# Four plain block products at the entry of a ConvFFN, a swapped transpose, and a norm and its squares in another place

## The chip, the cores and the metric

The kernel runs on one core of one Trainium2 chip. The metric is device time in microseconds (us), lower is better. An execution's own time holds its profiled span and about 2 us around it. The engines: PE (TensorE, matmuls), DVE (VectorE), ACT (ScalarE), POOL (GpSimd) and SP (SyncE, which issues the DMAs). PSUM is the memory that matmuls write.

## The reference

A two-layer streaming encoder step on 1056 tokens (1024 of a prompt, 32 of a sample), width 1024. Layer 0 mixes with an HGRN2 gated recurrence of 8 heads, layer 1 with differential attention. What matters here is what stands around the mixer `m` in each layer:

```
x = x + rmsnorm(m, g_norms[i, 1])
h = rmsnorm(x, g_norms[i, 2])
g, u = split(h @ w_ffn_in[i])              # 1024 -> 2 * 2816
c = conv_b + conv_w[0]*g[t-2] + conv_w[1]*g[t-1] + conv_w[2]*g[t]
f = (silu(c) * u) @ w_ffn_out[i]           # 2816 -> 1024
x = x + rmsnorm(f, g_norms[i, 3])
x = x + sigmoid(x @ w_ple_gate[i]) * (ple[i] @ w_ple[i])
```

`rmsnorm` divides by the root of a mean of squares over the 1024 features of a token. After layer 0, x is normed again and projected to the keys and values that layer 1 reads.

## The kernel before, in words

**Products.** Activations stand feature-major: eight tiles of 128 features by tokens. Every float32 factor is split in a rounded high part (ACT casts, L169) and the rest (DVE subtracts, L170; L110 and L111 for weight pieces of 1024 columns), and a product is three matmuls: high by high, low by high, high by low (L120 to L122). Weights come by DMA into a `raw` tile and are split into `ws` slabs. Tokens go in groups of 384, 384 and 288 (t = 0, 1, 2), in the FFN in two halves of 528, each in two pieces of 264.

**The mixer's output** (`mixer_out`, both layers). A unit (t, j) is the product for one feature tile j of token group t; its PSUM is added to a partial sum by DVE (L304), or for t = 2 copied by ACT (L302). ACT then squares it and POOL adds the square into `acc` (L195 to L203). `norm_m(t)` turns the sum into a factor with a matmul by ones (L190) and two ACT operations, multiplies the eight tiles (L318), adds the residual (L319) and squares again into `xacc`; `norm_x(t)` multiplies by that second factor (L331) and writes the `y` tiles, the FFN's input. PE's order here is written out by hand: the units, with the norms' ones-matmuls between them, and behind them `ple`, the product of the per-layer embedding, which needs none of the norms. The order on the other engines comes from a scheduler, which sets an instruction as early as its inputs are there, by priority.

**The FFN's entry** (`operands`, `weights7`, `ffn_in`). Input and weights are cut into two by two blocks, and each of the 22 blocks of 128 FFN rows (ft) takes seven products in the manner of Strassen and Winograd instead of eight. The input's seven operands are four blocks or sums of them (b1, b2, b3 and b6, b7, b5, b4), made once per layer by DVE (L432, L433, L434, L439) and split by ACT and DVE; the seven weight operands are made for each ft. A product is 24 matmuls of 264 columns. Results leave PSUM by ACT copies (L513, L528) and DVE adds (L505). `raw` has two buffers for these weights, there are ten slabs, and PSUM pools of 3 (`psd`), 4 (`psm`) and 1 (`psr`).

**The FFN's end** (`ffn_out`). `post` norms f, `gate` multiplies the embedding by a sigmoid and adds (L629 to L636), and `store(t)` splits the new x for the next layer and squares it into `xacc`, whose ones-matmul (L181) gives the factor of the next norm.

**The HGRN heads** (`gla`, layer 0). Each head ends its score stage with the 32 tokens of the sample: a 32x32 matmul into PSUM tile `ps` (L987), a masked copy of it by DVE (L988), a transpose of the keys by PE into another part of the same tile (L989), and an ACT copy of that (L991).

Of the kernel before, what the change touches and what calls it, by code (L numbers as in the profile page):

```python
# [18 lines left out]
P = 128  # L19
# [27 lines left out]
class Trunk:  # L47
# [228 lines left out]
    def mixer_out(self, l, wsrc, gpost, resid, yp):  # L276

        nc, tc, io = self.nc, self.tc, self.io
        with tc.tile_pool(name=self.nm("mo"), bufs=1, reuse_waits="tile") as mp:
# [6 lines left out]
            for ks in ((4, 5, 6, 7), (0, 1, 2, 3)):  # L286
                for i in (1, 2):
                    for k in ks:
                        y[k][i] = yp.tile([P, YT[i][1]], F32, tag=f"y{k}{i}", name=self.nm("y"))
            for k in range(KD):  # L290
                y[k][0] = yp.tile([P, YT[0][1]], F32, tag=f"y{k}0", name=self.nm("y"))
            g_in = self.G(4 * l + 2)

            def unit(t, j):
# [39 lines left out]
            with tc.manual_schedule(engines={mybir.EngineType.PE}):  # L334
                for t, j in [(t, j) for t in range(3) for j in range(KD)]:
# [50 lines left out]
    def layer_end(self, l, wsrc, gpost, resid, last):  # L386

        tc = self.tc
        with self.phase("ff", 1, 2, m=4, r=1) as fp:
            with tc.tile_pool(name=self.nm("yp"), bufs=1, reuse_waits="tile") as yp:  # L390
# [4 lines left out]
                w = self.weights7(l, 0)  # L395
                b = next(b)
            with tc.tile_pool(name=self.nm("rp"), bufs=1, reuse_waits="tile") as rp:
                ready = self.ffn_in(l, w, b, fp, rp)
# [6 lines left out]
    def operands(self, y):  # L405
# [5 lines left out]
        def alloc(op, ps):  # L411
            for p in ps:
                out[p] = [[op.tile([P, HT], F32R, tag=f"b{p}{k}{i}", name=self.nm(f"b{p}")) for i in range(2)]
                          for k in range(4)]
# [5 lines left out]
        def b(kh, hf, k, i):  # L420
            return y[4 * kh + k][1 + i] if hf else y[4 * kh + k][0][:, parts[i]]

        def put(p, kh, hf, i=None):
            for k in range(4):
                c = slice(0, HT) if i is None else parts[i]
                self.split(y[4 * kh + k][0] if i is None else b(kh, hf, k, i), *[o[:, c] for o in out[p][k]])

        def sums(i):
            put(3, 1, 1, i)
            for k in range(4):  # L430
                b11, b12, b22 = b(0, 0, k, i), b(0, 1, k, i), b(1, 1, k, i)
                nc.vector.tensor_tensor(b11, b12, b11, SUB)  # L432
                nc.vector.tensor_tensor(b12, b22, b12, SUB)  # L433
                nc.vector.tensor_tensor(b22, b22, b11, SUB)  # L434
# [954 lines left out]
```

## Time and profile before

| | |
|---|---|
| median of 3 runs | 3009.33 us (2995.96 to 3010.63) |
| the profiled execution's own time | 3011.07 us |
| its span | 3009.3 us |
| PE busy | 2906.3 us, 97% |
| DVE busy | 2001.6 us, 67% |
| ACT busy | 1299.2 us, 43% |
| POOL busy | 283.8 us, 9% |
| mean granted TensorE clock | 0.983 |

A busy PE is not PE at its full clock: the granted clock of a stretch stands beside its busy time. Where PE is idle the trace names what it waited for last. The core is one, so the span is the time but for the 2 us around it.

### The profile page before, as it was taken

What the parts mean: (1) busy time and instruction counts of PE and PEld (TensorE: products, weight loads), DVE (VectorE), ACT (ScalarE), POOL (GpSimd) and SP (SyncE); (2) the same over time, 40 slices, a digit from 0 to 9 for tenths busy, and PEclk for the clock granted to TensorE, in tenths of its full rate; (3) what the DMA queues carried; (4) which work ended last, traced back from release to release, by engine and by line L of the source; (5) the groups of instructions that cost most, each with busy time, mean ns of one, the idle gap of its engine ahead of it and who ended that gap; (6) DMA issues with size and microseconds to landing.
All of it is one profiled execution on the core that took longest, in us unless ns stands there. A gap on an engine that the chain in (4) does not pass through costs nothing.

```text
span 3009.3 us, 50595 instructions
## 1 busy us (share of the span) xinstructions
PE 2906.3 (97%) x20302; PEld 2798.5 (93%) x20302; DVE 2001.6 (67%) x3874; ACT 1299.2 (43%) x2355; POOL 283.8 (9%) x431
## 2 busy tenths in 40 slices
PE   8999999988999999999989999999889999999999
PEld 8889999978999999998988888989889999999989
DVE  7556555488777766667657575575887777767674
ACT  6445435464343333115436454565643333331151
POOL 0000000140000000003321111001400000000020
PEclk9999999999999999999999999999889999999999
DMA  3111111351222224334232232232512222242242
GB/s 133 46 39 41 53 47 60 103 172 64 85 72 79 85 79 137 124 117 148 87 107 77 84 92 81 90 105 74 184 57 79 79 79 79 83 152 86 86 148 70
DMA packets 105013, 275.34 MB, mean 91 GB/s; under 512 B 12241, under 2 KB 49225, under 8 KB 104777
## 3 DMA queue, kind: packets, MB, share of 16 engines
q1 hardware_dynamic: 102216, 263.71, 26.2%
q0 software_dynamic: 2560, 8.39, 1.4%
q8 instruction: 159, 2.61, 0.4%
q14 instruction: 78, 0.63, 0.1%
HBM read 196.53 MB, written 71.86 MB: 89 GB/s over the span
## 4 chain that ended last, share of the span: by engine, by line
PE 85%; DVE 8%; ACT 3%; issue 1%; DMA 1%; POOL 1%; SPq 0%; DVEq 0%; ACTq 0%; POOLq 0%
PE psm L122 14%; PE psm L120 14%; PE psm L121 14%; PE psd L120 11%; PE psd L121 11%; PE psd L122 11%; PE po L1233 1%; DVE b L170 1%; PE pss L1199 1%; PE psm L1225 1%; PE pss L1200 1%; DVE ws L111 1%; DVE x L170 1%; PE po L1235 1%; PE po L181 1%
## 5 line engine op out<-in xcount | busy, mean ns | idle before, releaser
L120 PE MATMUL psd<-x,ws 128*128 128x384 f32 (+1 forms) x1512 | 518.9, 343 | 17.7 <-ACT x L681 9.9
L120 PE MATMUL psm<-b,ws 128*128 128x264 f32 x1760 | 502.2, 286 | 4.4 <-ACT y L528 2.5
L122 PE MATMUL psm<-b,ws 128*128 128x264 f32 x1760 | 503.7, 287 | 2.2 <-DVE ws L170 2.2
L121 PE MATMUL psm<-b,ws 128*128 128x264 f32 x1760 | 502.7, 286 | 2.8 <-DVE b L170 2.8
L121 PE MATMUL psd<-x,ws 128*128 128x384 f32 (+1 forms) x1512 | 498.5, 330 | 0.0
L122 PE MATMUL psd<-x,ws 128*128 128x384 f32 (+1 forms) x1512 | 494.4, 327 | 1.3 <-DVE ws L111 1.3
L121 PE MATMUL psm<-y,ws 128*128 128x384 f32 (+1 forms) x1056 | 342.5, 325 | 5.6 <-DVE y L170 5.6
L120 PE MATMUL psm<-y,ws 128*128 128x384 f32 (+1 forms) x1056 | 343.7, 326 | 0.4 <-DVE f L612 0.3
L122 PE MATMUL psm<-y,ws 128*128 128x384 f32 (+1 forms) x1056 | 341.2, 324 | 0.0
L120 PEld LDWEIGHTS psm<-b,ws 128*128 128x128 f32 x1760 | 333.5, 190 | 5.8 <-ACT y L528 3.0
L121 PEld LDWEIGHTS psm<-b,ws 128*128 128x128 f32 x1760 | 333.7, 190 | 3.5 <-DVE b L170 3.5
L122 PEld LDWEIGHTS psm<-b,ws 128*128 128x128 f32 x1760 | 333.4, 190 | 2.6 <-DVE ws L170 2.6
L169 ACT CAST ws<-raw 128x512 fp32r<-128x512 f32 x308 | 191.1, 621 | 326.1 <-DVE raw L479 105.3
L612 DVE TENSOR_TENSOR f<-psm,f 128x384 f32<-128x384 f32 (+1 forms) x432 | 221.1, 522 | 153.5 <-PE psm L122 152.4
L120 PEld LDWEIGHTS psd<-x,ws 128*128 128x128 f32 x1512 | 288.8, 191 | 30.4 <-ACT x L681 10.1
L121 PEld LDWEIGHTS psd<-x,ws 128*128 128x128 f32 x1512 | 288.9, 191 | 6.8
L122 PEld LDWEIGHTS psd<-x,ws 128*128 128x128 f32 x1512 | 288.3, 191 | 6.7 <-issue 3.2
L170 DVE TENSOR_TENSOR ws<-raw,ws 128x512 fp32r<-128x512 f32 x308 | 211.2, 697 | 114.6 <-ACT ws L169 114.6
L111 DVE TENSOR_TENSOR ws<-raw,ws 128x1024 fp32r<-128x1024 f32 (+1 forms) x138 | 166.6, 1208 | 93.3 <-ACT ws L110 93.0
L120 PE MATMUL psd<-b,ws 128*128 128x264 f32 x704 | 200.1, 285 | 17.0 <-ACT b L169 17.0
L121 PEld LDWEIGHTS psm<-y,ws 128*128 128x128 f32 x1056 | 199.6, 189 | 7.8 <-DVE y L170 7.0
L120 PEld LDWEIGHTS psm<-y,ws 128*128 128x128 f32 x1056 | 199.4, 189 | 2.5 <-DVE f L612 1.0
(303 smaller groups left out, 6093.4 us busy)
## 6 DMA issues: line engine op xcount, KB each, us to landing
raw<-wfi SPq DMA_DIRECT2D x88, 512.0 KB, 3.3
hd<-y SPq DMA_DIRECT2D x44, 528.0 KB, 2.7
raw<-wfo SPq DMA_DIRECT2D x44, 512.0 KB, 4.4
rh<-hd SPq DMA_DIRECT2D x40, 528.0 KB, 3.7
raw<-wia SPq DMA_DIRECT2D x30, 512.0 KB, 3.4
ped<-pe SPq DMA_DIRECT2D x16, 528.0 KB, 2.8
y<-ped SPq DMA_DIRECT2D x16, 528.0 KB, 4.8
raw<-wpg SPq DMA_DIRECT2D x16, 512.0 KB, 4.3
```

Of the source, the lines that this page charges most:

```text
L111: nc.vector.tensor_tensor(wl[:, w], raw[:, w], wh[:, w].bitcast(F32), SUB)
L120: mm(ps, wh, xh, start=start and i == 0, stop=False, skip_group_check=more)
L121: mm(ps, wh, xl, start=False, stop=False, skip_group_check=more)
L122: mm(ps, wl, xh, start=False, stop=stop and i == n - 1, skip_group_check=more)
L169: self.nc.scalar.copy(hi, src)
L170: self.nc.vector.tensor_tensor(lo, src, hi.bitcast(F32), SUB)
L181: nc.tensor.matmul(ps, self.ones, acc, start=True, stop=True)
L612: nc.vector.tensor_tensor(f[j][t], ps, f[j][t], ADD)
L1199: mm(ps[:, :pad], qs[c][:, P * i:P * i + P], kh[c][:, k0:k0 + pad], start=True, stop=False)
L1200: mm(ps[:, :pad], qs[c][:, P * i:P * i + P], kl[c][:, k0:k0 + pad], start=False, stop=True)
L1225: nc.tensor.transpose(ps[:, i * P:i * P + P], ws[a][:, kt * P:kt * P + P], self.ident)
L1233: mm(po, v[:, 2 * b, :], wts[b][:, 0:256], start=b == 0, stop=False)
```

## The change

- **Entry.** Block ft = 0 is computed as eight plain block products (four blocks for the gate, four for the up rows), on operands b1, b2, b3 and b5 alone; gate and up rows have PSUM tiles and copies of their own. Its weights are two plain pieces in four slabs, and the seven operands of ft = 1 are loaded before it. The other 21 blocks keep the seven products.
- **Operands.** The four feature tiles of a block lie in one tile, so a split or a subtraction is one instruction over 2112, 960 or 1152 elements. The splits of b1 and b2 have high priority, and the sums come in another order: b5 first, then b6, b7, b4.
- **Mixer's output.** The evacuations of `unit` have high priority; `norm_x(0)` stands behind unit (2, 3) instead of (1, 7).
- **Rows.** The FFN's rows are eight named tiles, taken in turn, instead of a pool of eight.
- **FFN's end.** The squares for the next norm are made in `gate`, not in `store`; for the last two feature tiles of t = 2 DVE adds them instead of POOL; `store(2)` has high priority.
- **Short chunk.** The transpose is issued ahead of the masked copy.

```diff
--- mixer_out
                 if t == 2:
                     nc.tensor.matmul(ps, self.ident, m, start=False, stop=True)
                     m = y[j][2]
-                    nc.scalar.copy(m, ps)
-                else:
-                    nc.vector.tensor_tensor(m, ps, m, ADD)
                 with tc.high_priority():
+                    if t == 2:
+                        nc.scalar.copy(m, ps)
+                    if t < 2:
+                        nc.vector.tensor_tensor(m, ps, m, ADD)
                     self.sumsq(acc[t], m, j == 0, mp)
...
-                    if (t, j) == (1, 7):
-                        norm_x(0)
                     if (t, j) == (2, 1):
                         norm_m(1)
+                    if (t, j) == (2, 3):
+                        norm_x(0)
--- layer_end
-                w = self.weights7(l, 0)
+                w = [self.piece(self.io["wfi"][l, i]) for i in (0, NFF)]
+                w1 = self.weights7(l, 1)
--- operands
-        put(1, 0, 0)
-        put(2, 1, 0)
-        sums(0)
-        sum4(0)
-        yield
-        sums(1)
+        with self.tc.high_priority():
+            put(1, 0, 0)
+            put(2, 1, 0)
+        put(3, 1, 1, 0)
+        yield
         self.opb = self.right("opb", 1)
         alloc(self.opb, (7, 5, 4))
+        put(3, 1, 1, 1)
+        sub((0, 0), (0, 1), (0, 0))
+        put(5, 0, 0)
+        sub((0, 1), (1, 1), (0, 1))
+        sub((1, 1), (1, 1), (0, 0))
+        for i in range(2):
+            put(6, 1, 1, i)
+        sub((1, 0), (1, 0), (1, 1))
         for i in range(2):
             put(7, 0, 1, i)
-        put(5, 0, 0)
-        sum4(1)
         put(4, 1, 0)
--- ffn_in, block ft = 0
+                gp, u = row(), row()
+                halo(gp, cv)
+                X, Y = ([self.psm()[:, 0:HT // 2] for _ in range(2)] for _ in range(2))
+                Z, W = ([(self.psd() if m == "d" else self.psm(m))[:, 0:HT // 2] for m in mk] for mk in ("dd", "dr"))
...
+                block(0, 0, 1, X)
+                copies([(p1[:, n], X[s]) for s, n in enumerate(pieces)])
+                block(1, 0, 1, Y)
+                copies([(q1[s], Y[s]) for s in range(2)])
+                block(0, 1, 2, X, more=True)
+                block(1, 1, 2, Y, more=True)
+                block(0, 1, 3, Z)
+                block(1, 1, 3, W)
+                block(0, 0, 5, Z, more=True)
+                block(1, 0, 5, W, more=True)
+                copies([(gp[:, 2 + n.start:2 + n.stop], X[s]) for s, n in enumerate(pieces)])
+                copies([(u[:, n], Y[s]) for s, n in enumerate(pieces)])
+                u2 = p1
+                for s, n in enumerate(pieces):
+                    add(u[:, HT + n.start:HT + n.stop], W[s], q1[s])
--- ffn_out, gate and store
             nc.sync.dma_start(dst[j][:, t0:t0 + n], f[j][t])
+            if not last:
+                self.sumsq(self.acc[t], f[j][t], j == 0, f2, nc.vector if t == 2 and j >= 6 else None)
...
-                self.store_x(t, j, f[j][t], self.acc[t], f2)
+                self.store_x(t, j, f[j][t], None, f2)
--- rows of ffn_in and ffn_out
-            return rp.tile([P, T + 4], F32, tag="y", name=self.nm("y"), bufs=8)
+        self.nrow += 1
+        return pool.tile([P, T + 4], F32, tag=f"y{self.nrow % 8}", name=self.nm("y"), bufs=1)
--- gla
         mm(ps[0:32, 0:32], kd[:, SEQ:T], qd[:, SEQ:T], start=True, stop=True)
+        nc.tensor.transpose(ps[0:32, P:2 * P], kc[:, SEQ:T], self.ident)
         nc.vector.copy_predicated(A[0:32, SEQ:T], tri[0:32], ps[0:32, 0:32])
-        nc.tensor.transpose(ps[0:32, P:2 * P], kc[:, SEQ:T], self.ident)
```

Lines of the changed kernel are shifted (L304 is L306, L318 and L319 are L319 and L320, L331 is L332, L989 is L1025, and both copies of PSUM at the entry of block 0 are L501).

PE at the short chunk of a head in layer 0, before. `psm_951` is the tile that the 32x32 product and the transpose share; `psd_965` belongs to a projection of the next head.

```order
L122 MATMUL psd_897<-x_65_217,ws_712 128x384
L987 MATMUL psm_951<-qd_596,d_517 32x32
L989 MATMUL psm_951<-ident,f_483 32x128 [waits DMAHW5_49,DVE_49]
L999 MATMUL psm_957<-ident,f_483 128x128 x4
L120 MATMUL psd_965<-x_18_123,ws_711 128x288
L121 MATMUL psd_965<-x_19_124,ws_711 128x288
```

The same place after:

```order
L122 MATMUL psd_897<-x_65_217,ws_712 128x384
L1024 MATMUL psm_951<-qd_596,d_517 32x32
L1025 MATMUL psm_951<-ident,f_483 32x128 [waits DMAHW5_49]
L1036 MATMUL psm_957<-ident,f_483 128x128 x4
L120 MATMUL psd_965<-x_18_123,ws_711 128x288 [waits DVE_49]
L121 MATMUL psd_965<-x_19_124,ws_711 128x288
```

The order of PE's instructions is the same; the transpose no longer waits for DVE, and a wait for DVE (an earlier one, for the PSUM buffer of `psd_965`) stands two instructions later.

DVE in `mixer_out` of layer 0 before, from the end of `norm_m(0)` (L318, L319) over the evacuations of units of t = 1 (L304, one per `psd`) to the first multiplication of `norm_x(0)` (L331):

```order
L318 SCALAR_TENSOR_TENSOR x_663_4987<-x_663_4987,gc,psm_5674 128x384
L319 TENSOR_TENSOR x_659_4965<-x_659_4965,x_842_5708 128x384
L318 SCALAR_TENSOR_TENSOR x_715_5276<-x_715_5276,gc,psm_5674 128x384
L319 TENSOR_TENSOR x_663_4987<-x_663_4987,x_844_5716 128x384
L318 SCALAR_TENSOR_TENSOR x_717_5291<-x_717_5291,gc,psm_5674 128x384
L304 TENSOR_TENSOR x_687_5093<-psd_5757,x_687_5093 128x384
L319 TENSOR_TENSOR x_715_5276<-x_715_5276,x_846_5724 128x384
L319 TENSOR_TENSOR x_717_5291<-x_717_5291,x_848_5732 128x384
L304 TENSOR_TENSOR x_690_5118<-psd_5774,x_690_5118 128x384
L304 TENSOR_TENSOR x_692_5138<-psd_5791,x_692_5138 128x384
L304 TENSOR_TENSOR x_719_5306<-psd_5808,x_719_5306 128x384
L331 SCALAR_TENSOR_TENSOR y_5497<-x_645_4864,gc,psm_5842 128x384
```

The same place after, up to the first multiplication of `norm_m(1)` (`psm_5859`):

```order
L306 TENSOR_TENSOR x_687_5093<-psd_5739,x_687_5093 128x384
L320 TENSOR_TENSOR x_647_4886<-x_647_4886,x_818_5666 128x384
L319 SCALAR_TENSOR_TENSOR x_649_4915<-x_649_4915,gc,psm_5656 128x384
L319 SCALAR_TENSOR_TENSOR x_655_4943<-x_655_4943,gc,psm_5656 128x384
L306 TENSOR_TENSOR x_690_5118<-psd_5756,x_690_5118 128x384
L320 TENSOR_TENSOR x_649_4915<-x_649_4915,x_820_5674 128x384
...
L306 TENSOR_TENSOR x_721_5321<-psd_5807,x_721_5321 128x384
L320 TENSOR_TENSOR x_717_5291<-x_717_5291,x_830_5714 128x384
L111 TENSOR_TENSOR ws_5477<-raw_5475,ws_5476 128x1024
L319 SCALAR_TENSOR_TENSOR x_667_5011<-x_667_5011,gc,psm_5859 128x384
```

The evacuations stand between the operations of `norm_m(0)` instead of behind them, and `norm_m(1)` follows at once, with `norm_x(0)` behind it.

ACT from the end of block 0 to the start of block 1 of the FFN in layer 0, before. `b_...` are operands, `ws_...` weight slabs, `y_6607` is the gate's row of block 0, `p_1034` the copy of block 1's first product.

```order
L169 CAST b_1007_6536<-y_5503 128x528
L169 CAST b_1009_6538<-y_5504 128x528
L528 COPY y_6607<-psm_6580 128x264
L528 COPY y_6607<-psm_6581 128x264
L169 CAST ws_6793<-raw_6786 128x512
L169 CAST ws_6792<-raw_6786 128x512
L169 CAST ws_6790<-raw_6785 128x512
L169 CAST ws_6795<-raw_6785 128x512
L513 COPY p_1034_6840<-psm_6814 128x264
```

The same place after. `b_955` is b4's high part, `ws_6394` the last slab of ft = 1, `raw_6883` a weight tile of ft = 2, `y_6448` and `y_6449` the gate's and up's rows of block 0.

```order
L169 CAST b_908_6194<-y_5483 128x4x288
L169 CAST ws_6394<-raw_6384 128x512
L169 CAST b_955_6420<-y_5485 128x2112
L169 CAST ws_6887<-raw_6883 128x512
L169 CAST ws_6889<-raw_6883 128x512
L501 COPY y_6448<-psm_6452 128x264
L501 COPY y_6449<-psm_6454 128x264
L501 COPY y_6448<-psm_6453 128x264
L501 COPY y_6449<-psm_6455 128x264
L501 COPY p_974_6704<-psm_6678 128x264
```

The copies that empty block 0's first PSUM tiles stand behind b4's cast and behind two casts of weights of ft = 2; `psm_6678`, the first product of block 1, uses the PSUM buffer that `y_6448<-psm_6452` empties.

## Rows read from the trace of the kernel before

**Rows 1.** Page, busy us of each engine, share of the span, instructions

```profile
PE 2906.3 (97%) x20302; PEld 2798.5 (93%) x20302; DVE 2001.6 (67%) x3874; ACT 1299.2 (43%) x2355; POOL 283.8 (9%) x431
```

**Rows 2.** Waits of PE: line, engine and line waited for, us in total, times, longest

```profile
PE psd L120 <- ACT b L169: 17.0, 2, 8.5
PE psm L989 <- DVE A L988: 10.7, 8, 4.6
...
PE psd L120 <- DVE x L304: 7.2, 2, 3.6
PE psm L181 <- POOL xacc L203: 6.4, 1, 6.4
...
PE psd L120 <- ACT y L302: 5.1, 2, 2.6
...
PE psd L120 <- ACT pe L378: 3.7, 2, 1.9
PE psm L190 <- POOL acc L203: 3.0, 2, 1.5
```

**Rows 3.** Stretches: us, busy us (instructions) of five engines, granted clock, DMA

```profile
710.00:1110.00 400.00, 400.00 (x3280) 400.00 (x3279) 290.12 (x511) 156.27 (x255) 18.44 (x76) 1.00 0.22 78
1510.00:1515.00 5.00, 1.22 (x3) 0.94 (x4) 4.31 (x9) 3.93 (x7) 3.22 (x2) 0.50 0.39 146
155.00:160.00 5.00, 4.90 (x18) 4.80 (x19) 2.08 (x12) 3.22 (x5) 0.00 (x0) 0.50 0.00 0
160.00:165.00 5.00, 5.00 (x37) 5.00 (x36) 4.04 (x4) 3.34 (x5) 0.00 (x0) 0.89 0.00 0
90.00:95.00 5.00, 5.00 (x32) 4.98 (x31) 1.91 (x3) 4.21 (x5) 0.00 (x0) 0.72 0.00 0
635.00:640.00 5.00, 3.01 (x9) 2.38 (x10) 4.93 (x6) 2.97 (x8) 3.67 (x3) 0.55 0.32 95
680.00:690.00 10.00, 6.88 (x28) 6.26 (x29) 10.00 (x27) 5.47 (x13) 0.00 (x0) 0.50 0.11 41
```

**Rows 4.** Timeline of PE, `mixer_out` of layer 0 to block 1: start, us, [idle before]

```profile
617.53 0.81 PE L190 MATMUL psm<-acc,ones 128*128 128x384 f32 x2
...
666.03 0.28 PE L120 MATMUL psm<-b,ws 128*128 128x264 f32 x1
666.15 0.29 PE L121 MATMUL psm<-b,ws 128*128 128x264 f32 x1
...
705.01 0.29 PE L120 MATMUL psm<-b,ws 128*128 128x264 f32 x1
```

**Rows 5.** Timeline of DVE, the norms, then subtractions and splits at the entry, layer 0

```profile
615.09 3.24 DVE L331 SCALAR_TENSOR_TENSOR y<-x,gc,psm 128x384 f32<-128x384 f32 x6 [1.62 <-ACT psm L192]
618.25 1.22 DVE L111 TENSOR_TENSOR ws<-raw,ws 128x1024 fp32r<-128x1024 f32 x1
...
632.97 1.10 DVE L319 TENSOR_TENSOR x<-x,x 128x384 f32<-128x384 f32 x1 [0.94 <-DMA x<-xT]
...
644.19 0.94 DVE L318 SCALAR_TENSOR_TENSOR y<-y,gc,psm 128x288 f32<-128x288 f32 x2
...
676.46 1.35 DVE L439 TENSOR_TENSOR y<-y,y 128x240 f32<-128x240 f32 x4
...
690.94 1.56 DVE L439 TENSOR_TENSOR y<-y,y 128x288 f32<-128x288 f32 x4
692.41 2.56 DVE L170 TENSOR_TENSOR b<-y,b 128x528 fp32r<-128x528 f32 x4
694.89 0.69 DVE L170 TENSOR_TENSOR ws<-raw,ws 128x512 fp32r<-128x512 f32 x1
```

**Rows 6.** Timeline of ACT, casts of operands at the entry, layer 0

```profile
691.47 2.23 ACT L169 CAST b<-y 128x528 fp32r<-128x528 f32 x4 [5.70 <-issue]
...
705.94 0.38 ACT L513 COPY p<-psm 128x264 f32<-128x264 f32 x1 [1.25 <-PE psm L122]
```

**Rows 7.** Page, DMA issues: queue, count, KB each, median us from issue to landing

```profile
raw<-wfi SPq DMA_DIRECT2D x88, 512.0 KB, 3.3
```

More of the change, by code (lines that the diff above doesn't have):

```diff
@@ L285, in mixer_out @@
             y = [[None] * 3 for _ in range(KD)]
[L286 to L291, printed above, removed]
+            self.y3 = {}
+            for i in (1, 2, 0):
+                for kh in (1, 0):
+                    g = self.y3[kh, i] = yp.tile([P, 4, YT[i][1]], F32, tag=f"y{kh}{i}", name=self.nm("y"))
+                    for k in range(4):
+                        y[4 * kh + k][i] = g[:, k, :]
             g_in = self.G(4 * l + 2)
@@ L481, in weights7, with row, ffn_in, copies @@
         return out
-    def ffn_in(self, l, a, b, fp, rp):
+    def row(self, pool):
+        self.nrow += 1
+        return pool.tile([P, T + 4], F32, tag=f"y{self.nrow % 8}", name=self.nm("y"), bufs=1)
+    def ffn_in(self, l, w0, a, b, fp, rp):
         nc, tc = self.nc, self.tc
         pieces = [slice(0, HT // 2), slice(HT // 2, HT)]
+        n0, n1 = pieces
+        e = SEQ - HT - n1.start
         def row():
-            return rp.tile([P, T + 4], F32, tag="y", name=self.nm("y"), bufs=8)
+            return self.row(rp)
+        def copies(pairs):
+            with tc.high_priority():
+                for out, ps in pairs:
+                    nc.scalar.copy(out, ps)
+        def halo(gp, cv):
+            nc.gpsimd.memset(gp[:, 0:2], 0.0)
+            nc.gpsimd.tensor_copy(gp[:, 1026:1028], cv[:, 4:6])
         for ft in range(NFF):
-            a = self.weights7(l, ft) if ft else a
+            a = self.weights7(l, ft) if ft > 1 else a
             cv = self.ffc[:, l, ft, :]
@@ L500, in prod @@
                     self.mm3(ps[s], [(w[:, k * P:k * P + P], w[:, 512 + k * P:512 + k * P + P],
-                                      b[p][k][0][:, n], b[p][k][1][:, n]) for k in range(4)], not more, True, more)
+                                      b[p][0][:, k, n], b[p][1][:, k, n]) for k in range(4)], not more, True, more)
             def add(out, ps, other):
@@ L505, in add @@
                     nc.vector.tensor_tensor(out, ps, other, ADD)
-            X = [self.psm()[:, 0:HT // 2] for _ in range(2)]
-            prod(1, X)
-            p1 = fp.tile([P, HT], F32, tag="p1", name=self.nm("p1"))
-            gp = row()
-            with tc.high_priority():
-                for s, n in enumerate(pieces):
-                    nc.scalar.copy(p1[:, n], X[s])
-            nc.gpsimd.memset(gp[:, 0:2], 0.0)
-            nc.gpsimd.tensor_copy(gp[:, 1026:1028], cv[:, 4:6])
-            Y = [self.psm()[:, 0:HT // 2] for _ in range(2)]
@@ L517, in ffn_in @@
-            uu = row()
-            u2, u3 = uu[:, 0:HT], uu[:, HT:T]
-            for p in (2, 6) if ft == 0 else (6, 2):
-                if p == 6:
-                    prod(6, Y)
-                    for s, n in enumerate(pieces):
-                        add(u2[:, n], Y[s], p1[:, n])
-                else:
-                    prod(2, X, more=True)
-                    with tc.high_priority():
-                        for s, n in enumerate(pieces):
-                            nc.scalar.copy(gp[:, 2 + n.start:2 + n.stop], X[s])
@@ L581, in row @@
         def row():
-            return fp.tile([P, T + 4], F32, tag="y", name=self.nm("y"), bufs=8)
+            return self.row(fp)
         def post(t):
@@ L663, in ffn_out @@
                 if fin:
-                    store(2)
+                    with tc.high_priority():
+                        store(2)
     def load_x(self, gp):
```

81 lines of the change are left out of this document (46 added, 35 removed).

## The prediction

> **What bounds the kernel now.** I read the busy times first, then the waits of PE, then the granted clock of the stretches where those waits lie, then the timelines there. PE is busy for 97% of the span [rows 1], so only two things can move the time: the number of its matmuls, and the stretches in which it is idle or slow. In the middle of the FFN it is busy for 400.00 of 400 us at full clock, in the first row of [rows 3]; nothing is to be had there. The idle time is in a list of places [rows 2], and the change goes to four of them: the transpose of the short chunk (10.7 us, eight heads), the mixer's output (7.2 + 5.1 + 3.7 + 3.0 = 19.0 us over both layers), the FFN's entry (17.0 us from its largest wait alone) and the norm between the layers (6.4 us). An idle PE costs more than the wait: the stretches right behind these waits are granted 0.50 to 0.55 of the clock [rows 3], which is the lower of the two levels, 1.2 GHz for 2.4.
>
> **Short chunk.** No instruction is added or removed. The transpose waited for a masked copy with which it shares only the PSUM tile, and that copy stood in DVE's queue behind long operations, 4.6 us in the worst head [rows 2]. In the new order of PE the transpose waits for a DMA alone, and the next wait for DVE is for the buffer of a projection's PSUM, whose evacuation stands earlier in DVE's queue. Gone: 10.7 us of idle time. The clock: behind the worst wait PE works 4.90 us at 0.50 and 5.00 at 0.89, behind the next one 5.00 at 0.72 [rows 3]; the loss is 2.45 + 0.55 + 1.4 = 4.4 us. Together 15.1. I take -14, since the DVE operations of the head keep their own times and may be late for a later matmul; bounds -16 (some clock that I have not counted) and -8 (half of it comes back), and 0 as a rival.
>
> **Mixer's output, each layer.** No work is added on PE. Before, PE waits 3.6 us for an evacuation which stands behind all of `norm_m(0)`, 2.6 for a copy by ACT, 1.5 for POOL's last square and 1.9 for a copy of the embedding: 9.6 us, of 19.0 for two layers [rows 2]. With the clock (3.01 us at 0.55 in 635 to 640 alone, a loss of 1.4 [rows 3]; I estimate 4.5 in all, three times this row) 14 us is the most that can go. What follows from the order: evacuations between the norm's operations end the first wait, so the ones-matmul of t = 1, now at 617.53 [rows 4], comes about 4 us earlier, and so does `norm_m(1)`, whose end is at about 634 [rows 5]. Behind it now stand `norm_x(0)` (3.24 us for six of its eight operations, 4.3 for all) and two splits of 1.22 [rows 5]: 634 - 4 + 4.3 + 2.4 = 636.7. There `norm_m(2)` can start, which starts at 644.19 [rows 5]: 7.5 us earlier. The first operand and with it the entry follow that chain, at 658.5 instead of 666.03 [rows 4]. So -7.5 per layer, -15 for two; bounds 0 (residual and embedding arrive by DMA no earlier than now; one wait of 0.94 for that stands inside `norm_m(1)` [rows 5]) and -14 per layer.
>
> **FFN's entry, each layer.** Before: from 666.03 to 705.01, 39.0 us [rows 4], for seven products of 24 matmuls at 0.122 (two rows at 666 start 0.12 apart [rows 4]), which is 20.5 us; 18.5 us are waits for operands, and the half clock behind them (6.88 us of work at 0.50 from 680 to 690 [rows 3]). After: eight products, 8 x 24 x 0.122 = 23.4 us, so +24 matmuls and +2.9 us. They need four operands instead of seven in that time. Operand work gets a little shorter: four operations on 240, 288 or 528 elements take 1.35, 1.56 and 2.56 us [rows 5], the merged ones by estimate 1.1, 1.3 and 2.3 (three starts less each). DVE at the new entry: `norm_x(2)` ends about when the entry starts (T), with 2 us of exchange between ACT and DVE behind it (estimate); then nine operations on 512 elements at 0.66 between starts (0.69 for one [rows 5]), 5.9 us, a split of 1152 elements 1.3, three subtractions 3.6, and b5's cast (2.23 for four tiles [rows 6]) and split 2.3. The sum is T + 17; b5 is wanted after six products, at T + 17.6. It is just in time, and b3, before all of that, is early.
>
> So PE reaches the end of block 0 at about T + 23.4. There I see a new wait. The first product of block 1 takes over the PSUM buffer that ACT's copy of the gate's first piece empties, and that copy stands in ACT's queue behind b4's cast and two casts of weights of ft = 2. Those weights need a `raw` buffer, which comes free when DVE has split the last slab of ft = 1 (`ws_6394`). On DVE that split stands behind b6, b4's two subtractions and b7's first part: after b5 there are 1.1 + 1.3 + 1.1 + 1.1 + 1.3 + 1.3 + 1.1 + 0.7 = 9.0 us, so T + 26. Then comes a DMA of 3.3 us [rows 7] with 0.4 to issue it, two casts of about 0.62 (the 528-wide ones start 0.53 apart [rows 6]) and the copy, 0.38 [rows 6]: T + 31.6. PE waits 8.2 us and works some us at half clock behind it, which I put at 2.0: 33.6 in place of 39.0, -5.4 per layer, -10.8 for two. What is queued behind ACT's waiting casts is all four copies of block 0 and block 1's first; PE waits for each of them. The bounds: if DVE splits that slab as soon as its operands allow, at T + 21.8 (the eighth of the products is then still running), the stretch ends at T + 27.3 and the gain is 11.7, and without any wait 15.6; if it takes until T + 34, the stretch is about 42 and the loss 3. I take the middle, since the order of DVE gives each step.
>
> In the trace ACT's operations start in the order in which they are issued, and a copy of PSUM that waits 1.25 us stands idle at the head of the engine [rows 6]. The Trainium skill ("TensorE: Matmul & The Clock Gate", the section on the 16 sub-arrays) says that ScalarE's queue is a strict FIFO: nothing passes a waiting instruction. By that rule the 8.2 us stand; if a copy could pass the casts, block 1 would start at T + 23.4, and the forecast would be 20 us lower for both layers. No row of before has a PSUM copy behind a cast that waits for a DMA, so it is the changed kernel that decides.
>
> **The norm between the layers.** The squares of t = 2 are made in `gate`, and DVE adds the last two. Before, PE is idle 6.4 us for POOL's sum [rows 2], then works at 0.50 (1510 to 1515 [rows 3]); I put that at 3, as much as behind the worst wait of the heads: 9.4 at most. After, 32 instead of 22 matmuls stand between the last gate and this ones-matmul. They need the low part of a key weight, and on DVE that stands behind seven splits of the last group: 7 x 0.39 (1.56 for four of that width [rows 5]) = 2.7, then 1.2 for the weight and some 0.8 of exchange, a wait of 4.7. I take -5; bounds -9.4 and 0.
>
> **The sum.** -14 - 15 - 10.8 - 5 = -44.8 on the profiled execution's 3011.07, which is 1.7 us above the median of the runs: 2966.3, or 2965 by the median. Rows by name, the high priority of `store(2)` and merged splits cost nothing as long as the middle of the FFN has no wait [rows 3]; DVE is busy 290 of 400 us there. Added up, the bounds of the terms are -84 (16 + 28 + 31 + 9) and -2 (8 less twice 3).
>
> **Rivals.**
> 1. The new wait at block 1 eats the entry: the chain through DVE, DMA and ACT ends at T + 36 or so, the entry gains nothing, and the mixer's output gains half. -14 - 7.5 - 0 - 4 = -25.5: 2984. For it: in 670 to 690 DVE is busy for all of 20 us [rows 3], so any delay there adds up. Against it: four operands are needed in place of seven.
> 2. Everything fits, with no wait at block 1: -15 - 22 - 28 - 8 = -73, 2936. For it: the sums of durations leave only 8 us to make up. Against it: the order in ACT's queue.
> 3. The swap at the short chunk does not do what it says, the wait moves to the next matmul that needs DVE: 2966.3 + 14 = 2980. For it: DVE's long operations are not shortened. Against it: PE has no other wait in the heads near that size [rows 2].
> 4. The other side: the rows by name. A tile by name is free only when the very row eight places back has been read, while a pool could give any buffer that was free. If block after block PE or DVE waits p us for its row, 42 blocks with seven products pay 42p. It takes over the gain of 44.8 from p = 1.1, and the kernel is slower by over 0.5% from p = 1.4; at p = 2 it is 3050. For it: each block still takes two or three of the eight rows, and the rows go out by DMA. Against it: no wait at all in the middle of the FFN [rows 3], so the slack is there, and eight rows are as many as before.
>
> **How the numbers follow.** Forecast (each term near its value, 2950 to 2980): 0.52. Rival 1: 0.20. Rival 2: 0.15. Rival 3: 0.06. Rival 4: 0.07. The range of 2934 to 2996 takes in rivals 1 and 3 and nearly all of 2; outside are rival 4, the lower part of rival 2 and the outer end of rival 1, about 0.17. A measurement of this kernel can tell 0.5% from no change, about 15 us, so faster means below 2994: the first three cases and most of rival 1, 0.87. Within 0.5%: 0.08, from the far end of rival 1 and rival 4 with p near 1. Slower: 0.05.
>
> **What would show it.** Right: no wait of PE at the transpose; 48 more matmuls; the wait for the evacuation in the mixer's output gone, and the entry's first matmul about 20 us before 666 in the trace (the heads' 14 and the mixer's 7.5); from there to the first product of block 1 about 33 us, with one wait of some 8 us for an ACT copy at its end; a ones-matmul between the layers that waits less than 3 us. Wrong: a wait for b5 or b3 inside block 0, a stretch at the entry near 24 or over 39 us, or waits in the middle of the FFN.

## The result and the profile after

The changed kernel takes 2962.39 us (median of 4 runs, 2957.72 to 2965.32), the kernel before 3003.55 beside it (2995.96 to 3010.63). The ratio is 0.9862 with a 95% interval of 0.9828 to 0.9896. The forecast was 2965. The profiled executions are 3011.07 and 2960.87 us, 50.2 apart. Executions at a far lower granted clock are left out of all medians, ratios and stretches, among them one with seven products at block 0 (3666.17 us, clock 0.714) and the profiled one with four embedding buffers alone (3988.73 us, clock 0.654).

To see where they part, I laid four marks on PE's timeline in both traces: the first ones-matmul of the mixer's output (L190), the first matmul on the entry's operands, the first matmul of block 1, and the matmul for the attention's bias (L1092 before, L1129 after), which comes ahead of the attention's weights. Each number is the difference of two starts. The first column runs from the first matmul of the kernel to the first mark, the last stretch from the bias matmul to the first transpose in the attention. Before, and with seven products, six matmuls of block 1 already stand ahead of the mark at block 1 (0.7 us), so those stretches are longer by that much.

| kernel | heads | ones-matmul to block 1, layer 0 | the same, layer 1 | bias to attention | median us |
|---|---|---|---|---|---|
| before | 584.2 | 110.9 (71.9 + 39.0) | 113.6 (73.2 + 40.5) | 361.5 | 3003.55 |
| after | 572.3 | 98.5 (74.0 + 24.5) | 97.2 (72.7 + 24.5) | 352.6 | 2962.39 |
| transpose behind the copy again | 582.5 | 98.6 | 98.1 | 354.1 | 2970.53 |
| mixer's output as before | 570.7 | 98.0 | 96.6 | 350.5 | 2964.64 |
| seven products at block 0 | 570.7 | 107.6 | 109.1 | 357.8 | 2979.45 |
| raw buffers by name | 572.2 | 99.7 | 99.8 | 347.4 | 2965.93 |
| ten squares on DVE | 572.4 | 93.9 | 94.3 | 351.4 | 2952.47 |
| gate's squares in store | 572.6 | 98.7 | 96.8 | 359.4 | 2963.08 |
| rows from a pool | 572.3 | 98.3 | 95.2 | 354.3 | 2958.36 (one run) |
| ten squares, four embedding buffers | 572.6 | 93.5 | 92.3 | 349.4 | 2950.40 |
| ten squares, mixer's order as before | 572.3 | 94.5 | 96.3 | 351.1 | 2956.23 |
| gate's squares all on POOL | 572.8 | 96.5 | 97.9 | 355.1 | 2963.07 (one run) |
| ten squares, four buffers and b4 first | 570.7 | 90.8 | 90.5 | 352.1 | 2950.16 |

The waits of PE in the changed kernel (us in total, times, longest), to be laid beside [rows 2]:

```profile
PE psm L190 <- POOL acc L203: 12.3, 4, 3.8
PE psd L120 <- ACT x L718: 9.7, 1, 9.7
PE psd L120 <- ACT pe L379: 7.6, 4, 3.4
...
PE psm L120 <- ACT y L501: 2.0, 2, 1.0
PE psm L1062 <- ACT vn L1052: 1.9, 1, 1.9
PE psd L120 <- ACT y L304: 1.6, 2, 0.8
```

The 17.0 us for an operand's cast, the 10.7 of the transpose, the 7.2 for the evacuation and the 6.4 for POOL between the layers are gone. New are 12.3 us for POOL's sums in the mixer's output, where 3.0 stood, and 7.6 for the embedding's rows, where 3.7 stood. The 9.7 us for x are the kernel's start, as before.

PE's timeline of the second head, changed kernel, where before it waited 4.6 us:

```profile
149.37 0.25 PE L1024 MATMUL psm<-qd,d 128*32 128x32 f32 x2
149.55 0.28 PE L1025 MATMUL psm<-ident,f 128*32 128x128 f32 x1
149.67 0.60 PE L1036 MATMUL psm<-ident,f 128*128 128x128 f32 x4
150.02 0.42 PE L120 MATMUL psd<-x,ws 128*128 128x384 f32 x1
```

The transpose follows at once, and so does the projection behind it.

PE's timeline of the mixer's output and the entry, layer 0, changed kernel; it answers to [rows 4]. The bracket is the idle time before and what ended it.

```profile
601.84 1.28 PE L190 MATMUL psm<-acc,ones 128*128 128x384 f32 x2 [2.35 <-POOL acc L203]
...
620.39 0.40 PE L120 MATMUL psd<-ple,ws 128*128 128x288 f32 x1 [0.79 <-ACT y L304]
...
625.26 1.33 PE L190 MATMUL psm<-acc,ones 128*128 128x288 f32 x2 [3.81 <-POOL acc L203]
...
640.56 0.69 PE L120 MATMUL psd<-ple,ws 128*128 128x384 f32 x1 [3.24 <-ACT pe L379]
...
655.98 0.28 PE L120 MATMUL psm<-b,ws 128*128 128x264 f32 x1
...
680.49 0.39 PE L120 MATMUL psm<-b,ws 128*128 128x264 f32 x1 [0.99 <-ACT y L501]
```

From 655.98 PE runs through eight products without a wait, and block 1 starts 24.5 us later after one of 0.99. The mixer's output in front of it has as much waiting as before, on other engines: 12.3 + 7.6 + 1.6 = 21.5 us over both layers, where it was 19.0. POOL's end of the sums there:

```profile
615.00 1.13 POOL L203 TENSOR_TENSOR acc<-acc,sq 128x288 f32<-128x288 f32 x1
616.10 1.01 POOL L203 TENSOR_TENSOR xacc<-xacc,sq 128x384 f32<-128x384 f32 x1
617.07 1.12 POOL L203 TENSOR_TENSOR acc<-acc,sq 128x288 f32<-128x288 f32 x1
618.15 1.34 POOL L203 TENSOR_TENSOR xacc<-xacc,sq 128x384 f32<-128x384 f32 x1
619.45 0.79 POOL L203 TENSOR_TENSOR acc<-acc,sq 128x288 f32<-128x288 f32 x1
620.21 2.09 POOL L203 TENSOR_TENSOR xacc<-xacc,sq 128x384 f32<-128x384 f32 x2
622.25 2.95 POOL L203 TENSOR_TENSOR acc<-acc,sq 128x288 f32<-128x288 f32 x1
```

Two sums share POOL without a gap: the units' own (`acc`) and those of `norm_m(1)` (`xacc`). The last one ends at 625.2, and the ones-matmul starts there. That last addition is one of 128x288 and takes 2.95 us, where the same one takes 0.79 at 619.45. DVE beside it:

```profile
622.21 2.35 DVE L111 TENSOR_TENSOR ws<-raw,ws 128x1024 fp32r<-128x1024 f32 x2
629.86 0.94 DVE L319 SCALAR_TENSOR_TENSOR y<-y,gc,psm 128x288 f32<-128x288 f32 x2 [5.31 <-ACT psm L192]
```

DVE splits two weight pieces there, and then waits 5.31 us for the factor that hangs on POOL's sum. By these rows some 2 us of PE's 3.81 are the long last addition, and the rest is the queue in front of it.

ACT at the end of block 0, changed kernel, then SP's weight loads:

```profile
676.50 0.62 ACT L169 CAST ws<-raw 128x512 fp32r<-128x512 f32 x1 [2.95 <-PE psd L121]
677.11 1.97 ACT L169 CAST b<-y 128x2112 fp32r<-128x2112 f32 x1
678.98 1.18 ACT L169 CAST ws<-raw 128x512 fp32r<-128x512 f32 x2
680.06 1.21 ACT L501 COPY y<-psm 128x264 f32<-128x264 f32 x4
```

```profile
662.97 0.33 SPq L459 DMA_DIRECT2D raw<-wfi  x1
678.73 0.33 SPq L460 DMA_DIRECT2D raw<-wfi  x1
```

The copies do stand behind b4's cast and two casts of block 2's weights, but those weights were asked for at 662.97, 7 us into the entry, and none of the casts waits for a DMA. The load at 678.73 is the one that had to wait for the last slab, and no cast ahead of the copies reads it.

### The profile page after: what moved, and what is told of

Read it like the earlier page. It is cut to its first block, busy times and chain, and to the rows that moved or that the text cites. A ratio compares the mean times of both kernels' runs of the same rounds, so it can differ in the third digit from the quotient of the medians.

```text
span 2959.1 us, 50514 instructions
## 1 busy us (share of the span) xinstructions
PE 2892.9 (98%) x20350; PEld 2785.4 (94%) x20350; DVE 1971.6 (67%) x3738; ACT 1293.5 (44%) x2296; POOL 272.7 (9%) x429
## 4 chain that ended last, share of the span: by engine, by line
PE 86%; DVE 6%; ACT 3%; DMA 2%; issue 1%; POOL 1%; SPq 0%; DVEq 0%; ACTq 0%; POOLq 0%
PE psm L120 14%; PE psm L122 14%; PE psm L121 14%; PE psd L120 11%; PE psd L122 11%; PE psd L121 11%; PE po L1270 1%; PE pss L1236 1%; PE psm L1262 1%; PE pss L1237 1%; DMA raw<-wfo 1%; DVE ws L111 1%; DVE x L320 1%; PE po L1272 1%; PE po L181 1%
## 5 line engine op out<-in xcount | busy, mean ns | idle before, releaser
L120 PE MATMUL psm<-b,ws 128*128 128x264 f32 x1744 | 497.0, 285 | 2.0 <-ACT y L501 2.0
L122 PE MATMUL psm<-b,ws 128*128 128x264 f32 x1744 | 495.8, 284 | 0.0
L121 PE MATMUL psm<-b,ws 128*128 128x264 f32 x1744 | 495.8, 284 | 0.0
L120 PEld LDWEIGHTS psm<-b,ws 128*128 128x128 f32 x1744 | 327.8, 188 | 2.4 <-ACT y L501 2.4
L122 PEld LDWEIGHTS psm<-b,ws 128*128 128x128 f32 x1744 | 328.8, 189 | 0.0
L121 PEld LDWEIGHTS psm<-b,ws 128*128 128x128 f32 x1744 | 328.6, 188 | 0.0
L110 ACT CAST ws<-raw 128x1024 fp32r<-128x1024 f32 (+1 forms) x142 | 146.6, 1034 | 411.5 <-PE psm L121 295.4
L169 ACT CAST ws<-raw 128x512 fp32r<-128x512 f32 x294 | 182.6, 622 | 308.6 <-DVE raw L476 101.1
L170 DVE TENSOR_TENSOR ws<-raw,ws 128x512 fp32r<-128x512 f32 x294 | 198.6, 687 | 111.2 <-ACT ws L169 111.0
L111 DVE TENSOR_TENSOR ws<-raw,ws 128x1024 fp32r<-128x1024 f32 (+1 forms) x142 | 171.5, 1210 | 105.6 <-ACT ws L110 104.0
```

The source lines that it names most:

```text
L110: nc.scalar.copy(wh[:, w], raw[:, w])
L111: nc.vector.tensor_tensor(wl[:, w], raw[:, w], wh[:, w].bitcast(F32), SUB)
L120: mm(ps, wh, xh, start=start and i == 0, stop=False, skip_group_check=more)
L121: mm(ps, wh, xl, start=False, stop=False, skip_group_check=more)
L122: mm(ps, wl, xh, start=False, stop=stop and i == n - 1, skip_group_check=more)
L169: self.nc.scalar.copy(hi, src)
```

## The experiments

**The swap alone undone.**

```diff
-        nc.tensor.transpose(ps[0:32, P:2 * P], kc[:, SEQ:T], self.ident)
         nc.vector.copy_predicated(A[0:32, SEQ:T], tri[0:32], ps[0:32, 0:32])
+        nc.tensor.transpose(ps[0:32, P:2 * P], kc[:, SEQ:T], self.ident)
```

> The changed kernel with the short chunk's transpose behind the masked copy again, nothing else. Theory A (the swap takes away the waits and the half clock behind them, less a small part that comes back as a wait of 1.9 us for a copy by ACT in the second head): the stretch from the first matmul to the first ones-matmul of the mixer's output takes 584 us, as before, instead of 572.3 in the changed kernel, and the whole is 12 us slower, about 2973. Rival (the wait only moves, and the 12 us come from another part of the change): the stretch stays at 572 to 575 and the whole within 3 us of the changed kernel.

The heads take 582.5 us, and the wait is back as it was: eight times, 10.7 us in all, 4.6 the longest. The whole is 2970.53, 8 us slower. Theory A holds: the swap is worth 10.2 us in the heads, where 12 was expected; the kernels that have the swap differ by 2 us there (570.7 to 572.8).

**The mixer's edits undone.**

```diff
-                with tc.high_priority():
-                    if t == 2:
-                        nc.scalar.copy(m, ps)
-                    if t < 2:
-                        nc.vector.tensor_tensor(m, ps, m, ADD)
+                if t == 2:
+                    nc.scalar.copy(m, ps)
+                if t < 2:
+                    nc.vector.tensor_tensor(m, ps, m, ADD)
...
+                    if (t, j) == (1, 7):
+                        norm_x(0)
...
-                    if (t, j) == (2, 3):
-                        norm_x(0)
```

> The changed kernel with the evacuations of the mixer's units at their old priority and the norm of the first tokens at its old place. From the first ones-matmul of this stage to the first product of the entry before took 71.9 us in layer 0 and 73.2 in layer 1, the changed kernel 74.0 and 72.7. Theory B (what sets the end there is POOL's adding of squares and the DMAs of the embedding, which neither edit touches): undone, both stay at 72 to 75, the whole within 3 us of the changed kernel. Rival 1 (the edits do bring the forecast 7.5 us per layer, and the four weight tiles that are now loaded and split in this stage instead of two take them away again): undone, the stretches take about 80 us, the whole 15 us more. Rival 2 (the edits themselves harm): undone, the stretches are 3 us or more shorter.

The stretch up to the entry's first matmul falls to 65.2 and 63.8 us, but the entry then takes 32.8: PE's order here mixes the last embedding products with the first of the entry (36 of their matmuls stand behind the entry's first), so this mark moved with the work. By its letter the run shows rival 2's sign, a stretch 3 us or more shorter; up to block 1, which all of the work has to pass, it is 98.0 and 96.6 us, half a microsecond less than with the edits. They bring nothing here: the 7.2 us for the evacuation are back, and POOL's 12.3 fall to 5.6. That excludes rival 1, and rival 2 but for half a microsecond. Whether POOL is the reason was left to later runs.

**Seven products at block 0, with the merged tiles.**

```diff
-                w = [self.piece(self.io["wfi"][l, i]) for i in (0, NFF)]
-                w1 = self.weights7(l, 1)
+                w, w1 = None, self.weights7(l, 0)
...
-            if ft:
+            if True:
```

(with the sums and block 0's products in the order of before)

> The changed kernel with seven products again at block 0, in the order of before and with the sums in the order of before, but with the merged operand tiles. Theory C (the entry ends when the operands are there, and four operands in place of seven are the gain, the merged instructions a small part): from the first product to block 1's first 35 us per layer instead of 24.5, as the merged operations save about 4 of before's 39.0; the whole 21 us slower, about 2982. Rival (merging and priority do most of it): at most 28 us per layer, the whole 7 us slower at most.

107.6 and 109.1 us to block 1, so 9.1 and 11.9 more than with eight products; the whole is 2979.45, 17 us slower. From the entry's first matmul it is 40.6 and 40.8, where 35 was expected, but that mark comes 6.9 and 4.4 us earlier here than with eight products. Waits for casts of operands are back (9.9 and 6.2 us). Theory C holds in kind: most of the gain comes with the eight products. The remaining 3.3 and 4.5 us against before are not separated; merging and priority are among what makes them.

**Raw weight buffers in turn.**

```diff
-        return self.wp.tile([P, 1152], F32, tag="raw", name=self.nm("raw"), bufs=2)
+        self.nraw = getattr(self, "nraw", -1) + 1
+        return self.wp.tile([P, 1152], F32, tag=f"raw{self.nraw % 2}", name=self.nm("raw"), bufs=1)
```

> The changed kernel with the two raw weight buffers as two named tiles taken in turn, in place of a pool that gives the one that is free first. The forecast's wait at block 1 (8 us) did not come: there is one of 1.0 us. Theory D (the chain was right but for one link: the first weights of block 2 got the buffer that came free at 7 us after the entry's start, where the forecast had them wait for the other one, free at 22 us): with buffers in turn they wait for the later one, ACT's copies of block 0 stand behind them, and block 1 starts 31 to 32 us after the entry's start instead of 24.5, so 13 to 15 us more in all if the later blocks don't change. Rival (ACT's queue would not have held the copies back, whatever the buffer): block 1 starts within 1.5 us of 24.5.

ACT at the same place:

```profile
675.25 1.96 ACT L170 CAST b<-y 128x2112 fp32r<-128x2112 f32 x1
680.50 0.62 ACT L170 CAST ws<-raw 128x512 fp32r<-128x512 f32 x1 [3.29 <-DMA raw<-wfi]
681.03 1.21 ACT L502 COPY y<-psm 128x264 f32<-128x264 f32 x4
```

Now the cast waits 3.29 us for its DMA and the copies wait behind it; block 1's matmul on the buffer they empty starts at 681.46, 27.25 after the entry's start at 654.21, in place of 24.5. PE's two waits there:

```profile
680.73 0.39 PE L121 MATMUL psd<-b,ws 128*128 128x264 f32 x1 [3.01 <-DVE y L520]
681.46 0.39 PE L121 MATMUL psm<-b,ws 128*128 128x264 f32 x1 [0.21 <-ACT y L502]
```

Two matmuls of a later product of block 1 come first here, and they wait 3.01 us for DVE's addition that empties their buffer; the copy comes last, 0.21 us behind them. So the forecast's mechanism is there when its link is put in, and ACT's order does hold the copies back, but 7 us more were expected and the run shows 2.8, of which 2.0 would stand by DVE's addition alone. The load was issued at T + 22.6, not T + 26. The medians don't tell this apart from the changed kernel (2965.93 and 2962.39).

**Ten squares from POOL to DVE** (nine additions per layer, since the first square of a sum is not added).

```diff
-                    self.sumsq(acc[t], m, j == 0, mp)
+                    self.sumsq(acc[t], m, j == 0, mp, nc.vector if t == 2 or (t == 1 and j >= 6) else None)
```

> The changed kernel with the squares of the mixer's units added by DVE instead of POOL for the last two units of t = 1 and all of t = 2. In the changed kernel PE waits 2.35 and 3.81 us per layer for POOL's sums, before those waits were 0 and 1.5; from the first ones-matmul of the mixer's output to block 1 it takes 98.5 and 97.2 us. Theory B (the evacuations come earlier, but POOL adds one square after another, 1.0 to 1.4 us each, and now sets when the norms can start): without POOL both waits go, and with the half clock behind them 5 to 6 us per layer, to 92 or 93, the whole 10 us faster. Rival (DVE's ten more additions push back the evacuations and the norms by as much): 97 to 99 again, the whole within 3 us.

93.9 and 94.3 us, and the whole is 2952.47 (ratio to before 0.9827, 0.9808 to 0.9847). Theory B holds, a little short (92 or 93 us were expected): POOL's waits are gone, and 4.6 and 2.9 us with them. PE's waits in that stage now:

```profile
601.47 0.91 PE L190 MATMUL psm<-acc,ones 128*128 128x384 f32 x2 [1.16 <-DVE acc L203]
621.11 0.60 PE L120 MATMUL psd<-ple,ws 128*128 128x288 f32 x1 [3.33 <-ACT y L304]
636.87 0.44 PE L120 MATMUL psd<-ple,ws 128*128 128x384 f32 x1 [3.31 <-ACT pe L379]
676.59 0.39 PE L120 MATMUL psm<-b,ws 128*128 128x264 f32 x1 [2.50 <-ACT y L501]
```

**Four buffers for the embedding's rows** (`bufs=4` in place of `bufs=2` for `pe`).

> The changed kernel with four buffers instead of two for the rows of the embedding's product. PE waits 3.2 and 0.5 us per layer there for an ACT copy, which waits for a buffer whose DMA is queued on SP behind the residual's loads and stores of the third token group's norm. Theory (that queue is the second wait that took over from the evacuations): with four buffers the wait goes, and the stretch from the first ones-matmul to block 1 is 4 to 6 us shorter per layer, 93 to 94. Rival (the operands are no earlier, and PE then waits for b5 or for the first operand what it waited here): 97 to 99.

Inconclusive: no stretch can be read from its trace, and the other runs (2950.98 to 2964.23) lie as far apart as the effect.

**The gate's squares back in store.**

```diff
-            if not last:
-                self.sumsq(self.acc[t], f[j][t], j == 0, f2, nc.vector if t == 2 and j >= 6 else None)
...
-                self.store_x(t, j, f[j][t], None, f2)
+                self.store_x(t, j, f[j][t], self.acc[t], f2)
```

> The changed kernel with the squares for the next norm in store again, added by POOL, and store(2) at its old priority. From the first of the three ones-matmuls between the layers to the first transpose of the attention it took 64.3 us before and 54.9 in the changed kernel. Theory (this edit is worth all of it): 63 to 65 again, the whole 9 us slower. Rival (part of the 9.4 us comes from rows by name or from the smaller work on POOL): 59 or less.

58.0 us in the stretch I had named, which is the rival's side (59 or less): undone, the edit gives back 3.0 of the 9.4 us. PE also waits 2.2 us for a weight just ahead of the first ones-matmul, so at most some 5 are the edit's. POOL's sum is waited for 1.05 us, not the 6.4 of before [rows 2], so most of that wait went by something else; by what, no run here shows. From the bias matmul it is 359.4 against 352.6 of the changed kernel and 361.5 of before, but that can't be read: kernels that have the edit show 347.4 to 357.8 there. The medians (2963.08 and 2962.39) don't show an effect.

**Rows from a pool again.**

> The changed kernel with the rows of the FFN from a pool of eight again instead of eight names in turn. The changed kernel has two small waits at the start of layer 0's FFN output that before had not (1.3 and 0.7 us for an ACT copy, which stands behind an activation that waits for DVE), and none in the middle of the FFN. If the names make them, they go and nothing else moves (2 us); if not, they stay, and the names cost and bring nothing.

From block 1 to the bias matmul of the attention's weights 499.2 us, in the changed kernel 501.4, before 499.5. One wait of 0.37 us stands where two of 1.3 and 0.7 stood; but other kernels with the names show from under 0.2 to 2.1 there, and 498 to 504 in the stretch. This one execution shows no effect of the names.

**Ten squares and four buffers.**

> The changed kernel with both: squares of the mixer's last ten units added by DVE, and four buffers for the embedding's rows. With the squares alone the stretch from the first ones-matmul of the mixer's output to block 1 took 93.9 and 94.3 us, with PE waits of 3.4 for ACT's copy of a unit, 3.3 for a row of the embedding and 2.5 for ACT's copies of block 0; the whole was 2952. Theory (SP's queue is the next wait): the embedding's wait goes, the stretch is 90 to 92, the whole 2944 to 2949. Rival (ACT's copies of block 0 at the end wait for a chain that does not get shorter, as PE there only waits longer): 93 to 95 and the whole 2950 to 2954.

The embedding's wait is gone, and 93.5 and 92.3 us remain: one of 1.35 for b5's split and one of 4.27 for ACT's copies at block 1 took its place. The whole is 2950.40 (ratio 0.9819, 0.9800 to 0.9837), at the rival's edge.

**Ten squares, without the mixer's edits.**

> The kernel with the ten squares on DVE, but the evacuations' priority and the place of the first tokens' norm as before. With POOL in the way those two edits were worth nothing (98.5 and 97.2 us with them, 98.0 and 96.6 without). Theory (they were worth nothing because POOL's sums came last either way, so with the sums on DVE they count): without them the stretch is 97 us or more again, and the whole 6 us or more slower than 2952. Rival (they are worth nothing anyway, since the order on DVE only swaps one wait for another): 93 to 95, 2952.

94.5 and 96.3 us, 2956.23: between the two, nearer to the rival. With POOL out of the way the edits are worth 0.6 and 2.0 us per layer, so it is mostly as the rival says: 3.6 for the evacuation and 2.9 for a sum stand there against 3.3 for ACT's copy and 3.3 for the embedding.

**The gate's squares, all added by POOL.**

> The changed kernel with the squares for the next norm made in gate, but the last two of t = 2 added by POOL like the others. From the bias matmul before the attention's weights to its first transpose it took 361.5 us before, 352.6 in the changed kernel and 359.4 with the squares in store. Theory (making them at the gate is what counts, as POOL has nothing else left then): 352 to 354. Rival (the two additions on DVE matter): 356 or more, and a wait for POOL at the third ones-matmul.

355.1 us, between the two, in a stretch that varies by more (347.4 to 357.8). From the first of the three ones-matmuls to the attention it is 55.5 against 54.9; the third waits 1.22 us for ACT, none for POOL. So in this one execution the two additions on DVE are worth little.

**b4 first**, on top of the ten squares and the four buffers.

```diff
+        sub((1, 0), (1, 0), (1, 1))
+        put(4, 1, 0)
         for i in range(2):
             put(6, 1, 1, i)
-        sub((1, 0), (1, 0), (1, 1))
         for i in range(2):
             put(7, 0, 1, i)
-        put(4, 1, 0)
...
                 self.nrow = -1
+                for _ in range(6):
+                    self.row(rp)
```

> The kernel of the last comparison (ten squares on DVE, four buffers for the embedding's rows), and beside it b4 made and split right after b5, ahead of b6 and b7, and the rows of block 0 laid over the first block's input, which is free earliest. There PE waited 4.3 us at block 1 for ACT's copies of block 0, which stood behind b4's cast, and that behind b4's subtractions on DVE, 2.3 us after b6's first part. Theory (the operands that block 0 does not need set its end, through ACT's queue): b4's cast ends 2 to 3 us earlier and so does the wait, which is 1.5 to 2.5 us; the stretch from the first ones-matmul to block 1 is 90 to 91.5 us per layer instead of 93.5 and 92.3, the whole 2944 to 2948 instead of 2950. Rival (the copies are held by something else, or PE pays the same for b6 and b7, which are later): 92 to 94, 2950.

```profile
663.93 0.39 PE L121 MATMUL psd<-b,ws 128*128 128x264 f32 x1 [1.34 <-DVE b L170]
671.44 0.39 PE L120 MATMUL psm<-b,ws 128*128 128x264 f32 x1 [1.86 <-ACT y L503]
```

The wait at block 1 falls from 4.27 to 1.86, and the stretch to 90.8 and 90.5 us: theory. The whole is 2950.16 (2944.71 to 2953.51; ratio 0.9823, 0.9806 to 0.9840), like the kernel before it, so the 4.5 us of the stretches are not shown in the medians. The whole is on the rival's side, and the trace shows part of the reason: 8.4 us into block 1 PE now waits for another ACT copy, 0.8 us in layer 0 and 2.3 in layer 1, which it did not in the kernel before it. Both are about 12 us faster than the changed kernel, 0.4%.

## Why the prediction came out, and which steps did not

The time was right, and two of its four terms were far off: the mixer's output by +16.6 us and the entry by -19.7, over both layers. Nothing in the forecast said that these errors would cancel; that they did was luck. Of its own signs, two failed: the entry's first matmul came 10 us earlier, not 20, and "a stretch at the entry near 24" was named as a sign of being wrong, and it is 24.5. By the marks, in the profiled executions:

- **Short chunk**: forecast -14, measured -11.9. The mechanism is as forecast. A new wait of 1.9 us for ACT in the second head is the "late for a later matmul" that the term allowed for. Idle time of 10.7 us less that wait is 8.8; so the clock and the rest gave 3.1, or 1.4 by the swap undone (10.2), where 4.4 had been priced.
- **Mixer's output**: forecast -7.5 per layer, measured +2.1 and -0.4 up to the entry. The step that failed is "There `norm_m(2)` can start". I had followed DVE alone to that point. `norm_m(2)` needs the sum of the third group, and POOL adds 21 squares of the units and 14 of the first two norms one after the other; earlier evacuations and an earlier `norm_m(1)` only bring them to POOL's queue closer together. In [rows 2] POOL's share of the waits was 3.0 us, and I read it as a small wait that would go too; it was a queue with little to spare, and its last addition took 2.95 us in place of 0.8. The ten squares on DVE show that POOL's sums held the norms back: without them it is 4.6 and 2.9 us less to block 1. They don't show that POOL is all that ate the gain: with POOL out of the way the mixer's edits are still worth only 0.6 and 2.0 us, since a copy by ACT and a row of the embedding are waited for instead. The bound of 0 for this term was too good by 2 in layer 0.
- **Entry**: forecast -5.4 per layer, measured -14.5 and -16.0. Eight products and four operands are as forecast; b5 was even earlier, split by T + 14.0 in place of T + 17. The step that failed is "Those weights need a `raw` buffer, which comes free when DVE has split the last slab of ft = 1": the pool gave them the other one. The fourth rival's own words, that a pool gives any buffer that is free, would have told me. The run with buffers in turn shows the chain that I had described, at 2.8 us: even then the load is issued at T + 22.6 in place of T + 26, so its durations were put too high as well.
- **Norm between the layers**: forecast -5, measured -9.4 in the profiles (64.3 to 54.9), of which the edit undone gives back 3.0, at most some 5; what made the rest stays open. The wait of 4.7 us for the key weight was 0.9. The sizes of the operations were right, but DVE did seven of the store's splits while the last gate was still running (2.67 us from 1477.33), so they were not in the weight's way.

The rest is +1.9 in the rest of layer 0's FFN and -2.2 in the attention, two stretches that differ by 5 and 8 us between the runs here (498 to 504, 531 to 539), whatever the kernel. The sum is -50.2 between the profiled executions and -41 between the medians; the forecast was -44.8. Of the rivals the second described the entry ("with no wait at block 1"), but for the 0.99. The fourth did not come: the middle of the FFN has no wait.

Up to block 1 the two wrong terms belong together. From the first ones-matmul to block 1 I had forecast -12.9 per layer and the trace shows -12.4 and -16.4. As I read the rows, what sets the end of that stretch is one chain over DVE, POOL and ACT to the operands; a wait that is taken out of it in one place stands again further down, until the work in the chain gets less. Fewer operands made it less, and so did ten squares moved from POOL to DVE.

## What to carry to other kernels

When a wait is removed, follow every input of the next waiting instruction, the small engine's queue too: a wait of 1.5 us can be the end of a queue that is nearly full. Where a chain goes through a pool, find out which of its buffers an instruction gets, since the next load starts when that one comes free: 7 us into the entry here, or 22.6. A mark between two stages says little where the order lets work slip across it; measure to the next point that all of the work has to pass.

## What the runs showed of the hardware

DVE and POOL slow each other where both work on SBUF tiles (the memory beside PSUM that holds the activations and weights), which I had not priced. In `mixer_out` of layer 0 in the changed kernel, DVE's timeline and then POOL's:

```profile
588.17 0.54 DVE L320 TENSOR_TENSOR x<-x,x 128x384 f32<-128x384 f32 x1
...
590.15 2.56 DVE L320 TENSOR_TENSOR x<-x,x 128x384 f32<-128x384 f32 x2
```

```profile
607.70 0.80 POOL L203 TENSOR_TENSOR acc<-acc,sq 128x288 f32<-128x288 f32 x1 [2.76 <-ACT sq L202]
...
615.00 1.13 POOL L203 TENSOR_TENSOR acc<-acc,sq 128x288 f32<-128x288 f32 x1
```

The same DVE addition takes 0.54 us in a gap of POOL, or 1.28 where POOL's row is full; POOL's takes 0.80 beside DVE operations that read their factor from PSUM, 1.13 where such an addition overlaps it, and 2.95 beside two weight splits, as shown above. Over all traces but the one at low clock, DVE's addition of two such tiles takes 0.54 to 0.56 us in the 84 cases without POOL beside it; in the 167 with POOL beside it all the time it is 0.54 to 1.37, the median 1.09. With one input in PSUM (L306 in the changed kernel) it is 0.54 to 0.56 in all 416. Of POOL's 561 additions of 128x288, 20 took over 1.5 us, and 19 of these had a split of 1024 columns (L111) on DVE beside them. No run here was made to test this, so why they slow each other stays open. The medians of kernels whose stretches differ by 2 to 5 us can't be told apart, since the attention alone varies by more.
